# Moving the third sum of a Strassen group's tiles from VectorE to GpSimd, in a streaming-encoder block on one core

## The chip, the cores and the metric

The kernel runs on one core of one Trainium2 chip. The metric is device time in microseconds (us), the median of several runs. A core has five engines that run side by side and wait for each other through semaphores: TensorE (PE, with its weight loads PEld) multiplies matrices, VectorE (DVE) and ScalarE (ACT) work on tiles, GpSimd (POOL) does so too and issues some of the DMAs, SyncE (SP) issues the others. "128x1024" is a tile of 128 partitions by 1024 elements.

## The reference

One block of an encoder on 256 frames of width 2048, everything in float32: a half-step feed-forward layer, two token mixers beside each other (chunked attention and retention) merged by gates, a second half-step feed-forward layer, and a last norm.

```python
x = x + 0.5 * swiglu_ffn(rmsnorm(x, g1), ffn1_w_gate, ffn1_w_up, ffn1_w_down)   # 2048 -> 5632 -> 2048
h = rmsnorm(x, gm);  proj = h @ w_in                                             # 2048 -> 11264, nine parts
att = chunked_band_attention(q_a, k_a, v_a, rel_bias)
ret = silu(g_r) * chunkwise_retention(rotary(q_r), rotary(k_r), v_r)
merged = sigmoid(gate_a) * (att @ w_out_att) + sigmoid(gate_r) * (ret @ w_out_ret)
x = x + merged @ w_out
x = x + 0.5 * swiglu_ffn(rmsnorm(x, g2), ffn2_w_gate, ffn2_w_up, ffn2_w_down)
out = rmsnorm(x, gf)
```

## The kernel before

**Products in three parts.** Weights are streamed once, in chunks of 256 rows by 512 columns (`raw`, a 128x1024 tile). To keep float32 accuracy on TensorE, `split` makes two tiles of each chunk: `hi`, a rounded copy (ScalarE, line 126), and `lo`, the rest `raw - hi` (VectorE, line 127). `three` then multiplies hi by both parts of the activations (lines 137 and 138) and lo by the high part (line 140). So each chunk costs ScalarE one cast and VectorE one subtraction, and TensorE can't end the chunk's products before lo is there. At most four chunks (`SPLIT_BUFS`) are split ahead of TensorE.

**Strassen groups.** Two weight blocks of the same shape (the gate and up columns of a feed-forward block, or two gates of the mixer) are worked on together as 2 by 2 block matrices, in a form that spends 7 block products instead of 8 and pays for it with sums of weight chunks. There are 23 such groups: 9 in each feed-forward layer, 5 in the mixer. In a trace their tiles are named by a number: `z166k`, `z166x`, `loz16613s` belong to group 166. A group has four pairs of kept tiles, `k` and `x`, one pair for each of four slices `jc` of the inner dimension. Both are loaded by DMAs that GpSimd issues (line 539). The group goes through four phases. In phase 0 VectorE makes the first sum, x = x + k (line 528); in phase 1 the second, x = x + raw (line 583), where raw is a new chunk; then x is split (cast and subtraction, `hiz..1.s` and `loz..1.s`), and `third()` makes the third sum, k = x - k (line 570). After that GpSimd issues a DMA that loads one more chunk and adds it to x in memory (line 571), which becomes the x of phase 3. Phase 2 splits k, phase 3 splits x.

**Order.** The kernel writes its instructions in an order of its own (`weave`): steps of the groups alternate with chunks of ordinary products (`lo<-raw,hi` without a number), by shares written in a table. Each engine runs its instructions in that order and waits where a semaphore isn't there yet. Nothing reorders at run time. `third()` stands in `prep` of a phase 1 step, right behind the split of x.

Of the kernel before, what the change touches and what calls it, by code (L numbers as in the profile page):

```python
# [72 lines left out]
def block_kernel(ctx: ExitStack, tc: tile.TileContext, x, g1, w1g, w1u, w1d, gm, w_in, rel, woa, wor, wo,  # L73
                 g2, w2g, w2u, w2d, gf, cos, sin, decay, ident, out):
    nc = tc.nc
# [33 lines left out]
    def weights_tile(name):  # L109
        return wpool.tile([P, KC, NB], F32, tag="raw", bufs=RAW_BUFS, name=name)  # L110

    def chunk(w, r0, c0):
        return w[r0 : r0 + KC * P, c0 : c0 + NB].rearrange("(k p) n -> p k n", p=P)

    def fetch(t, w, r0, c0, parts=(slice(0, KC),)):
        for p in parts:
            nc.sync.dma_start(t[:, p, :], chunk(w, r0, c0)[:, p, :])
# [6 lines left out]
    def split(raw, name):  # L124
        hi, lo = split_tiles(name)
        nc.scalar.copy(hi, raw)  # L126
        nc.vector.tensor_sub(lo, raw, hi.bitcast(F32))  # L127
        return hi, lo
# [3 lines left out]
    def three(products, read_between=False):  # L132


        more = {"skip_group_check": True} if read_between else {}
        for acc, (ahi, alo), (whi, _), first, _ in products:
            nc.tensor.matmul(acc, ahi, whi, start=first, stop=False, **more)  # L137
            nc.tensor.matmul(acc, alo, whi, start=False, stop=False, **more)  # L138
        for acc, (ahi, _), (_, wlo), _, last in products:
            nc.tensor.matmul(acc, ahi, wlo, start=False, stop=last, **more)  # L140
# [372 lines left out]
    class Strassen:  # L513
# [43 lines left out]
        def step(self, phase, jc, of_sum):  # L557
            made = {}
            name = f"{self.name}{phase}{jc}{'rs'[of_sum]}"
            n = HALF_K // KC  # L560

            def load():
                made["raw"] = weights_tile(f"raw{name}")
                i = 2 - phase
                fetch(made["raw"], self.w[i], self.rows(1, jc), self.col[i])

            def third():

                x, k = self.x[jc], self.kept[jc]
                nc.vector.tensor_sub(k, x, k)  # L570
                nc.gpsimd.dma_start(x, chunk(self.w[0], self.rows(1, jc), self.col[0]), accum_op=ALU.add)

            def prep():
                x = self.x[jc]
                if not of_sum:
                    if phase == 0:
                        made["w"] = split(self.kept[jc], name)
                        self.first(jc)
                        return
                    raw = made.pop("raw")  # L580
                    made["w"] = split(raw, name)
                    if phase == 1:
                        nc.vector.tensor_add(x, x, raw)
                elif phase == 2:
                    made["w"] = split(self.kept.pop(jc), name)
                elif phase == 3:
                    made["w"] = split(self.x.pop(jc), name)
                else:
                    made["w"] = split(x, name)
                    if phase == 1:  # L590
                        third()

            bank, form, fresh, closing = {
# [4 lines left out]
            }[phase, of_sum]  # L598

            def products():  # L600
                hi, lo = made["w"]
                if fresh and jc == 0:
                    self.bank(bank)
                three([
                    (
                        self.acc[bank], self.norm.form(form, KC * jc + i), (hi[:, i, :], lo[:, i, :]),
                        fresh and jc == 0 and i == 0, closing and jc == n - 1 and i == KC - 1,
                    )
                    for i in range(KC)
                ], True)  # L610
                if jc == n - 1:
                    self.end(phase, of_sum)

            loaded = not of_sum and phase in (1, 2)
            frees = ["raw"] if loaded else ["kept"] if of_sum and phase > 1 else []
            return Step(self, 0, load if loaded else None, prep, frees, products)
# [641 lines left out]
```

## Time and profile before

| what | value |
|---|---|
| median of 3 runs | 2061.78 us (2060.89 to 2064.99) |
| the profiled execution | 2063.49 us, its span from first to last instruction 2061.4 us |
| TensorE clock granted | 0.999 of full speed |
| VectorE, ScalarE, GpSimd busy | 1754.4, 1402.9, 273.3 us |
| instructions of VectorE and GpSimd shown as busy | 1824 and 322 |
| the third sums, line 570 | 92 on VectorE, about 1.22 us each |

Times in a trace are counted from the first instruction. A row of the timeline gives the start, the duration, the engine, the line and the tiles as out<-in; "[4.44 <-DVE z166k L570]" says that the engine was idle for 4.44 us before it and that the instruction named ended that wait. Successive instructions of VectorE overlap a little: a 128x1024 sum is shown as 1.22 us, and the next one starts 1.13 to 1.14 us after it.

### The profile page before, as it was taken

What the parts mean: (1) busy time and instruction counts of PE and PEld (TensorE: products, weight loads), DVE (VectorE), ACT (ScalarE), POOL (GpSimd) and SP (SyncE); (2) the same over time, 40 slices, a digit from 0 to 9 for tenths busy, and PEclk for the clock granted to TensorE, in tenths of its full rate; (3) what the DMA queues carried; (4) which work ended last, traced back from release to release, by engine and by line L of the source; (5) the groups of instructions that cost most, each with busy time, mean ns of one, the idle gap of its engine ahead of it and who ended that gap; (6) DMA issues with size and microseconds to landing.
All of it is one profiled execution on the core that took longest, in us unless ns stands there. A gap on an engine that the chain in (4) does not pass through costs nothing.

```text
span 2061.4 us, 26148 instructions
## 1 busy us (share of the span) xinstructions
PE 2045.3 (99%) x9256; PEld 1691.9 (82%) x9256; DVE 1754.4 (85%) x1824; ACT 1402.9 (68%) x1732; POOL 273.3 (13%) x322
## 2 busy tenths in 40 slices
PE   9999999999999999999999999999999999999998
PEld 7788888888888888888888888888888878888886
DVE  7998899899997799899966667568989988998986
ACT  7677667777777767776665434556776677677785
POOL 1111211122111110122100000010122012110200
PEclk9999999999999999999999999999999999999999
DMA  8776876788678777788775645575787668876873
GB/s 308 207 225 230 269 227 207 239 264 258 191 231 258 240 205 251 258 284 260 227 267 175 223 143 187 187 245 170 235 273 234 200 224 273 240 206 233 281 215 133
DMA packets 219315, 473.28 MB, mean 230 GB/s; under 512 B 14816, under 2 KB 15568, under 8 KB 219184
## 3 DMA queue, kind: packets, MB, share of 16 engines
q1 hardware_dynamic: 161088, 309.89, 44.7%
q0 software_dynamic: 54752, 155.88, 27.9%
q10 hardware_dynamic: 3344, 5.84, 0.8%
q8 instruction: 72, 1.18, 0.2%
q14 instruction: 59, 0.48, 0.1%
HBM read 462.65 MB, written 8.91 MB: 229 GB/s over the span
## 4 chain that ended last, share of the span: by engine, by line
PE 93%; DVE 3%; DMA 2%; ACT 1%; issue 1%; SPq 0%; DVEq 0%; POOLq 0%; POOL 0%; ACTq 0%
PE acc L140 17%; PE acc L137 17%; PE acc L138 17%; DMA raw<-in_ffn_w_down_dram 2%; DVE lo L127 1%; ACT hi L126 0%; PE z684a L140 0%; PE z380a L137 0%; PE z953a L138 0%; PE z684a L138 0%; PE z418a L137 0%; PE z723a L138 0%; PE z380a L140 0%; PE z281a L138 0%; PE z723a L137 0%
## 5 line engine op out<-in xcount | busy, mean ns | idle before, releaser
L127 DVE TENSOR_TENSOR lo<-raw,hi 128x1024 fp32r<-128x1024 f32 x399 | 487.1, 1224 | 179.1 <-ACT hi L126 174.3
L126 ACT CAST hi<-raw 128x1024 fp32r<-128x1024 f32 x399 | 417.7, 1050 | 226.8 <-PE acc L138 143.7
L775 ACT ACTIVATE acc<-xall 128x512 f32<-128x512 f32 x96 | 57.5, 599 | 8.0 <-DVE f1g L742 3.6
L778 ACT ACTIVATE xall<-acc 128x512 f32<-128x512 f32 x96 | 56.6, 589 | 9.2 <-PE acc L140 7.4
L137 PE MATMUL acc<-hi,mgh 128*128 128x512 f32 x128 | 50.2, 392 | 0.0
L138 PE MATMUL acc<-hi,mgl 128*128 128x512 f32 x128 | 49.9, 390 | 0.0
L137 PE MATMUL acc<-hi,nma01h 128*128 128x512 f32 x96 | 38.7, 403 | 0.0
L137 PE MATMUL acc<-hi,nma00h 128*128 128x512 f32 x96 | 38.6, 402 | 0.0
L138 PE MATMUL acc<-hi,nma00l 128*128 128x512 f32 x96 | 37.5, 391 | 0.0
L137 PE MATMUL acc<-hi,nma10h 128*128 128x512 f32 x96 | 37.5, 391 | 0.0
L138 PE MATMUL acc<-hi,nma01l 128*128 128x512 f32 x96 | 37.5, 390 | 0.0
L138 PE MATMUL acc<-hi,nma11l 128*128 128x512 f32 x96 | 37.5, 390 | 0.0
L137 PE MATMUL acc<-hi,nma11h 128*128 128x512 f32 x96 | 37.4, 390 | 0.0
L138 PE MATMUL acc<-hi,nma10l 128*128 128x512 f32 x96 | 37.4, 390 | 0.0
L140 PE MATMUL acc<-lo,mgh 128*128 128x512 f32 x128 | 35.6, 390 | 0.0
L140 PE MATMUL acc<-lo,nma01h 128*128 128x512 f32 x96 | 29.6, 390 | 0.0
L140 PE MATMUL acc<-lo,nma00h 128*128 128x512 f32 x96 | 29.6, 390 | 0.0
L140 PE MATMUL acc<-lo,nma11h 128*128 128x512 f32 x96 | 29.6, 390 | 0.0
L140 PE MATMUL acc<-lo,nma10h 128*128 128x512 f32 x96 | 29.6, 390 | 0.0
L140 PEld LDWEIGHTS acc<-lo,mgh 128*128 128x128 f32 x128 | 24.0, 188 | 5.0
L137 PEld LDWEIGHTS acc<-hi,mgh 128*128 128x128 f32 x128 | 24.1, 188 | 4.9
L138 PEld LDWEIGHTS acc<-hi,mgl 128*128 128x128 f32 x128 | 24.1, 188 | 4.8
(6130 smaller groups left out, 6933.7 us busy)
## 6 DMA issues: line engine op xcount, KB each, us to landing
raw<-in_ffn_w_down_dram SPq DMA_DIRECT2D x176, 512.0 KB, 6.1
raw<-in_w_in_dram SPq DMA_DIRECT2D x96, 512.0 KB, 4.7
raw<-in_ffn_w_up_dram SPq DMA_DIRECT2D x32, 512.0 KB, 10.2
raw<-in_w_out_dram SPq DMA_DIRECT2D x32, 512.0 KB, 4.0
raw<-in_ffn_w_gate_dram SPq DMA_DIRECT2D x31, 512.0 KB, 5.9
raw<-in_w_out_att_dram SPq DMA_DIRECT2D x16, 512.0 KB, 4.3
raw<-in_w_out_ret_dram SPq DMA_DIRECT2D x16, 512.0 KB, 4.0
z380x<-in_w_in_dram POOLq DMA_DIRECT2D x8, 512.0 KB, 7.4
```

Source lines behind the costliest of these rows:

```text
L126: nc.scalar.copy(hi, raw)
L127: nc.vector.tensor_sub(lo, raw, hi.bitcast(F32))
L137: nc.tensor.matmul(acc, ahi, whi, start=first, stop=False, **more)
L138: nc.tensor.matmul(acc, alo, whi, start=False, stop=False, **more)
L140: nc.tensor.matmul(acc, ahi, wlo, start=False, stop=last, **more)
L775: nc.scalar.activation(acc, xs[t][:, cols], AF.Copy, scale=2.0)
L778: nc.scalar.activation(xs[t][:, cols], acc, AF.Copy, scale=0.5)
```

## The change

The third sum is given to GpSimd. It is the same subtraction on the same tiles, in the same place of the program.

```diff
             def third():

                 x, k = self.x[jc], self.kept[jc]
-                nc.vector.tensor_sub(k, x, k)
+                nc.gpsimd.tensor_sub(k, x, k)
                 nc.gpsimd.dma_start(x, chunk(self.w[0], self.rows(1, jc), self.col[0]), accum_op=ALU.add)
```

VectorE's order in phase 1 of group 166, its end (z166x and z166k are the group's kept tiles, the numbers behind them the buffers; loz1661.s the low parts of x, loz1661.r and rawz1661.r the new chunk; lo and raw a chunk of ordinary products):

```order
 L127 TENSOR_TENSOR loz16611s<-z166x_2702,hiz16611s 128x1024
-L570 TENSOR_TENSOR z166k_2690<-z166x_2702,z166k_2690 128x1024
 L127 TENSOR_TENSOR loz16613r<-rawz16613r,hiz16613r 128x1024
 L583 TENSOR_TENSOR z166x_2777<-z166x_2777,rawz16613r 128x1024
 L127 TENSOR_TENSOR lo_3061<-raw_2964,hi_3060 128x1024
 L127 TENSOR_TENSOR loz16612s<-z166x_2745,hiz16612s 128x1024
-L570 TENSOR_TENSOR z166k_2732<-z166x_2745,z166k_2732 128x1024
 L127 TENSOR_TENSOR loz16613s<-z166x_2777,hiz16613s 128x1024
-L570 TENSOR_TENSOR z166k_2759<-z166x_2777,z166k_2759 128x1024
 L127 TENSOR_TENSOR lo_3103<-raw_2978,hi_3102 128x1024
```

The sums are gone from VectorE's row and nothing takes their place; what stands behind each moves up.

GpSimd's order at the same place (L539 are loads of kept tiles, L571 the loads that add to x, z205k the next group's first kept tile):

```order
 L539 DMA z166x_2777<-in_ffn_w_gate_dram 128x2x512
+L570 TENSOR_TENSOR z166k_2616<-z166x_2642,z166k_2616 128x1024
 L571 DMA z166x_2642<-in_ffn_w_up_dram 128x2x512
+L570 TENSOR_TENSOR z166k_2690<-z166x_2702,z166k_2690 128x1024
 L571 DMA z166x_2702<-in_ffn_w_up_dram 128x2x512
+L570 TENSOR_TENSOR z166k_2732<-z166x_2745,z166k_2732 128x1024
 L571 DMA z166x_2745<-in_ffn_w_up_dram 128x2x512
+L570 TENSOR_TENSOR z166k_2759<-z166x_2777,z166k_2759 128x1024
 L571 DMA z166x_2777<-in_ffn_w_up_dram 128x2x512
 L539 DMA z205k_3174<-in_ffn_w_up_dram 128x2x512
```

Each sum now stands right ahead of the load that overwrites its x, and behind the load of the slice before. A sum on GpSimd needs x from line 583 only; the load behind it waits, as before, also for the cast and the subtraction that split x. The row of TensorE's instructions is the same in both kernels.

## The prediction

> **What bounds the kernel.** I read the page first (busy times, the chain that ended last), then the busy times by stage, then what TensorE waits for, then the timeline of VectorE around the sums. From the page:
>
> ```profile
> PE 2045.3 (99%) x9256; PEld 1691.9 (82%) x9256; DVE 1754.4 (85%) x1824; ACT 1402.9 (68%) x1732; POOL 273.3 (13%) x322
> ...
> PE 93%; DVE 3%; DMA 2%; ACT 1%; issue 1%; SPq 0%; DVEq 0%; POOLq 0%; POOL 0%; ACTq 0%
> ```
>
> TensorE is busy for 99% of the span and carries 93% of the chain. By stages, the Strassen groups lie in these (the first number behind the window is its length, then PE, PEld, DVE, ACT, POOL busy, the clock, the DMA share and GB/s); the last row is the 22 us around the sums of one group:
>
> ```profile
> 60.00:90.00 30.00, 28.39 (x125) 22.14 (x124) 30.00 (x29) 19.58 (x22) 6.30 (x7) 1.00 0.77 191
> 90.00:350.00 260.00, 259.94 (x1165) 214.86 (x1164) 239.05 (x222) 183.82 (x209) 39.21 (x46) 1.00 0.76 236
> 350.00:735.00 385.00, 384.25 (x1732) 317.63 (x1731) 337.83 (x337) 286.27 (x370) 59.28 (x69) 1.00 0.76 238
> 735.00:1035.00 300.00, 300.00 (x1337) 248.77 (x1336) 273.36 (x245) 210.85 (x226) 49.23 (x54) 1.00 0.83 254
> 1420.00:1990.00 570.00, 568.57 (x2543) 469.93 (x2542) 523.92 (x482) 408.98 (x472) 92.59 (x104) 1.00 0.78 237
> ...
> 337.00:359.00 22.00, 22.00 (x99) 18.22 (x98) 22.00 (x21) 15.41 (x18) 4.52 (x4) 1.00 0.87 235
> ```
>
> Two things are to be seen. TensorE is idle for only 1.61 + 0.06 + 0.75 + 0 + 1.43 = 3.85 us in all of these stages, so a lighter VectorE can give back about that. And around the sums VectorE is busy for 22.00 of 22.00 us: there it has no room at all. A busy TensorE may still be held up a little, since its ends are modelled; the waits of its weight loads show that better:
>
> ```profile
> PEld acc L140 <- DVE lo L127: 4.0, 8, 0.9
> PEld acc L137 <- ACT hi L126: 2.4, 3, 1.6
> ```
>
> These 6.4 us are the most that I allow as a gain. The timeline of VectorE in group 166, and the TensorE instruction that uses the last `lo` shown:
>
> ```profile
> 337.07 1.22 DVE L583 TENSOR_TENSOR z166x<-z166x,rawz16610r 128x1024 f32<-128x1024 f32 x1
> ...
> 341.61 1.22 DVE L127 TENSOR_TENSOR loz16610s<-z166x,hiz16610s 128x1024 fp32r<-128x1024 f32 x1
> 342.75 1.22 DVE L570 TENSOR_TENSOR z166k<-z166x,z166k 128x1024 f32<-128x1024 f32 x1
> 343.88 1.22 DVE L127 TENSOR_TENSOR loz16612r<-rawz16612r,hiz16612r 128x1024 fp32r<-128x1024 f32 x1
> ...
> 356.36 1.23 DVE L570 TENSOR_TENSOR z166k<-z166x,z166k 128x1024 f32<-128x1024 f32 x1
> 357.50 1.23 DVE L127 TENSOR_TENSOR lo<-raw,hi 128x1024 fp32r<-128x1024 f32 x1
> ...
> 359.16 0.62 PE L140 MATMUL acc<-lo,f1a1h 128*128 128x512 f32 x2
> ```
>
> From the first sum at 342.75 to the last at 356.36 every VectorE instruction is a subtraction or sum of two 128x1024 tiles in SBUF, one behind the other. The `lo` that starts at 357.50 ends at 358.73 and TensorE uses it at 359.16: VectorE is 0.43 us ahead. I call this distance the lead and looked for the shortest lead in and just behind the sums of each of the 23 groups. It is 1.99 us in the best (group 51), 0.05 in the worst, and 0.44 in the last; here the best, the first and the last:
>
> ```profile
> 147.54 1.23 DVE L127 TENSOR_TENSOR lo<-raw,hi 128x1024 fp32r<-128x1024 f32 x1
> 150.76 0.62 PE L140 MATMUL acc<-lo,f1a9h 128*128 128x512 f32 x2
> ...
> 74.21 1.22 DVE L127 TENSOR_TENSOR lo<-raw,hi 128x1024 fp32r<-128x1024 f32 x1
> 75.49 0.50 PE L140 MATMUL acc<-lo,n1a00h 128*128 128x512 f32 x1 [0.46 <-DVE lo L127]
> ...
> 1985.62 1.23 DVE L127 TENSOR_TENSOR lo<-raw,hi 128x1024 fp32r<-128x1024 f32 x1
> 1987.29 0.62 PE L140 MATMUL acc<-lo,f2a6h 128*128 128x512 f32 x2
> ```
>
> (147.54 + 1.23 = 148.77, used at 150.76: 1.99.) Over the 23 groups the shortest leads add up to 15.8 us, 0.69 on average. So whatever makes VectorE later by more than 0.69 us in a group's sums is paid by TensorE.
>
> **What the change removes.** 92 sums of VectorE. Each holds the next instruction back by 1.13 to 1.14 us (341.61, 342.75, 343.88 above); I take 1.135. That is 4.54 us in each group, 104 us in all. Taken alone it is worth little, because TensorE has only 3.85 to 6.4 us of waiting to give back. The largest piece lies in group 800, where the chain runs through a sum and a DMA that is issued late:
>
> ```profile
> 1647.39 1.09 DVE z800k L570
> ...
> 1650.82 11.20 DMA raw<-in_ffn_w_down_dram
> ```
>
> **What it adds on GpSimd.** The trace has no 128x1024 sum there. The nearest rows:
>
> ```profile
> L312 POOL MEMSET warm<- 128x512 f32 x1 | 0.5, 524 | 0.3 <-POOLq L1244 0.3
> ...
> L314 POOL MEMSET mhalf<- 128x4 f32 x1 | 0.1, 97 | 0.0
> ...
> L1115 POOL TENSOR_TENSOR frs<-v,mhalf 128x1 f32<-128x1 f32 x2 | 1.1, 559 | 66.2 <-DVE v L1113 66.2
> ...
> L373 POOL TENSOR_TENSOR rs<-v,mhalf 128x4 f32<-128x4 f32 x4 | 4.0, 1012 | 54.4 <-DVE v L372 54.4
> ```
>
> The fills give (524 - 97) / 508 = 0.84 ns for each element that passes. The powers of two inputs give (1012 - 559) / 3 = 151 ns for an element and 559 - 151 = 408 ns of start; the 151 belong to a power, I keep the start. Lower end: one element at a time at the speed of a fill, 0.86 + 0.10 = 0.96 us. Upper end: two reads and a write of each element one after the other, 2.58 + 0.41 = 2.99 us. I take two reads one after the other, 2 x 0.86 + 0.41 = 2.13 us, since the write can run beside the reads. [...]
>
> **GpSimd's queue.** The sums stand in front of the loads of line 571, and behind them the next group's loads:
>
> ```profile
> L571 POOL DMA_DIRECT2D z166x<-in_ffn_w_up_dram x4: 1194/1208/1240, 344.5 to 358.1; - x4
> ...
> z166x<-in_ffn_w_up_dram POOLq DMA_DIRECT2D x4, 512.0 KB, 6.4
> ...
> 360.72 1.06 ACT L126 CAST hiz16620s<-z166k 128x1024 fp32r<-128x1024 f32 x1 [0.58 <-PE acc L138]
> ...
> 372.99 1.04 ACT L126 CAST hiz16623s<-z166k 128x1024 fp32r<-128x1024 f32 x1
> ...
> 381.19 1.04 ACT L126 CAST hiz16633s<-z166x 128x1024 fp32r<-128x1024 f32 x1
> ```
>
> A slice costs GpSimd 2.13 + 1.21 = 3.34 us. The first sum may start at 338.3, when its x is done (337.07 + 1.22), and the last about where VectorE made it, near 356; its load is issued by about 359 and lands 6.4 us later, near 366. The last k is read at 372.99 and the last x at 381.19. So GpSimd may be some 15 us late before anyone waits. I cost its queue at nothing; without that cover each late us would go to ScalarE's cast and from there to TensorE.
>
> **Do the two engines hinder each other?** This decides the sign. Only one row has a GpSimd instruction of two inputs beside a VectorE one of two inputs:
>
> ```profile
> 19.38 1.23 DVE L127 TENSOR_TENSOR lo<-raw,hi 128x1024 fp32r<-128x1024 f32 x1
> 19.87 0.80 POOL L807 TENSOR_TENSOR there<-n1x,mhalf 128x4 f32<-128x4 f32 x1 [18.57 <-ACT n1x L462]
> ```
>
> A product of four elements takes 0.80 us and ends at 20.67, 0.06 us after the VectorE instruction (20.61). That is what a wait for VectorE's end would look like; it is one case, and start-up alone accounts for 0.41 us. Bounds of what a sum costs VectorE in waiting: 0 if they don't hinder each other, the whole sum if only one of them may read. I take the whole, 2.13 us, because this row is the only one of its kind. [...]
>
> **The sum.** A third sum then takes 1.135 us off VectorE and holds it up for 2.13: 0.995 later, 3.98 in a group. Less the shortest lead of each group that is 23 x 3.98 - 15.8 = 76 us. Four groups have a few VectorE instructions among the sums that read PSUM, or a pause of about 1 us; for a sum that falls there I take off 1 us each, 72 remain. The profiled execution (2063.5, that is 2.1 us around its span) is 1.7 above the median, 2061.8. So 2135.5 by its own time, 2134 beside the median. Ends of this case: with reads of 1.72 + 0.10 the group loses 2.74 and the sum is 47 us (2109); with 2.99 it is 155 (2217).
>
> **The rivals.**
> [...]
> - They don't hinder each other, and it gets faster. Speaking for it: the VectorE instruction at 19.38 kept its usual 1.23 us. TensorE then gets its 3.85 to 6.4 us back, group 800's late DMA first: 2055.4 to 2058. It decides at 1.135 us of waiting per sum: below that VectorE wins in every group, above it loses.
> - VectorE, which starts an instruction before the last one has ended, keeps GpSimd out until it pauses. The sums are pushed behind the cluster; the first k is due at 360.72, so ScalarE waits there for one sum, at most 2.13 us a group or 49 in all, less the lead that VectorE gained. 2060 to 2110.
>
> That the sums stay on VectorE is excluded by the order.
>
> **Chances.** Blocking 0.45 (2134, its own range 2100 to 2165), shared port 0.25 (2063 to 2099), no hindrance 0.18 (2055 to 2060), GpSimd kept out 0.12 (2060 to 2110). This kernel's runs can tell about 0.2%, 4 us, from no change. Faster by more: 0.14 of the third case and 0.01 of the last, 0.15. Within: 0.04, 0.05 of the shared port and 0.03 of the last, 0.12. Slower: 0.73. The range 2058 to 2165 leaves out most of the gain below and the long sums above, together about 0.2.
>
> **What would show it.** Line 570 has 92 rows on GpSimd of about 2.1 us, longer where they wait for VectorE. VectorE's lines 127 and 583 beside them are stretched to about 3.3 us or stand idle before; the lead is zero at the end of each group's sums, and TensorE waits for `lo` there, some 3 us a group, nothing elsewhere. [...] If line 570 takes over 3 us without waiting, only the size is wrong.

## The result, and the profile after

The changed kernel takes 2204.72 us (median of 4 runs, 2203.42 to 2206.36) against 2062.57 for the kernel before, a ratio of 1.0687 (95% interval 1.0672 to 1.0702). It is slower by 142 us. The sign was forecast; the time lies above the range of 2058 to 2165.

The page of the changed kernel, busy times, the chain that ended last, and the group of the ordinary chunks' `lo`; behind it the same group of the kernel before:

```profile
PE 2088.2 (95%) x9256; PEld 1704.7 (77%) x9256; DVE 1896.6 (86%) x1732; ACT 1400.8 (64%) x1732; POOL 590.1 (27%) x414
...
PE 81%; DVE 10%; issue 6%; DMA 1%; ACT 1%; DVEq 0%; ACTq 0%; POOLq 0%; POOL 0%
...
L127 DVE TENSOR_TENSOR lo<-raw,hi 128x1024 fp32r<-128x1024 f32 x399 | 562.6, 1413 | 174.4 <-ACT hi L126 168.3
```

```profile
L127 DVE TENSOR_TENSOR lo<-raw,hi 128x1024 fp32r<-128x1024 f32 x399 | 487.1, 1224 | 179.1 <-ACT hi L126 174.3 <-PE z684b L138 2.7 <-PE ro L981 1.0
```

VectorE has 92 instructions fewer (1824 to 1732) and is busy 142 us longer (1754.4 to 1896.6). TensorE falls to 95%, and VectorE's share of the chain grows from 3% to 10%. The same subtraction at line 127 takes 1413 ns on average instead of 1224. By stages:

```profile
90.00:350.00 260.00, 247.06 (x1076) 201.70 (x1075) 239.12 (x190) 169.00 (x191) 96.70 (x61) 0.98 0.75 226
350.00:735.00 385.00, 364.36 (x1577) 295.76 (x1576) 346.13 (x273) 261.73 (x312) 117.05 (x81) 0.98 0.72 215
735.00:1035.00 300.00, 283.85 (x1268) 231.12 (x1266) 276.89 (x234) 199.35 (x248) 99.48 (x65) 1.00 0.75 226
```

TensorE, which was idle for 0.06 us between 90 and 350, is now idle for 12.9 there, and the granted clock (the column behind POOL) is 0.98 in two of the stages. What it waits for:

```profile
PEld acc L140 <- DVE lo L127: 108.7, 60, 4.4
PE acc L140 <- DVE lo L127: 84.2, 50, 4.0
```

It waits for `lo`, as forecast: its weight loads do so 60 times instead of 8, for 108.7 us instead of 4.0. VectorE around the sums of group 166, and then GpSimd:

```profile
362.76 1.22 DVE L127 TENSOR_TENSOR loz16611r<-rawz16611r,hiz16611r 128x1024 fp32r<-128x1024 f32 x1
363.90 3.45 DVE L583 TENSOR_TENSOR z166x<-z166x,rawz16611r 128x1024 f32<-128x1024 f32 x1
367.27 1.21 DVE L127 TENSOR_TENSOR lo<-raw,hi 128x1024 fp32r<-128x1024 f32 x1
...
369.54 1.21 DVE L127 TENSOR_TENSOR loz16612r<-rawz16612r,hiz16612r 128x1024 fp32r<-128x1024 f32 x1
370.68 4.27 DVE L583 TENSOR_TENSOR z166x<-z166x,rawz16612r 128x1024 f32<-128x1024 f32 x1
374.87 1.21 DVE L127 TENSOR_TENSOR lo<-raw,hi 128x1024 fp32r<-128x1024 f32 x1
```

```profile
362.99 3.27 POOL L570 TENSOR_TENSOR z166k<-z166x,z166k 128x1024 f32<-128x1024 f32 x1 [25.16 <-ACT hi L126]
370.17 1.24 POOL L571 DMA_DIRECT2D z166x<-in_ffn_w_up_dram  x1 [3.91 <-DVE loz16610s L127]
370.95 2.90 POOL L570 TENSOR_TENSOR z166k<-z166x,z166k 128x1024 f32<-128x1024 f32 x1
```

The first sum waits for the VectorE instruction under way (it ends at 363.98) and runs to 366.26, 2.28 us. The next VectorE instruction shows 3.45 us instead of 1.22 and ends 1.09 us behind the sum (367.35). So it did nothing while the sum ran. At the second sum it is the same, with 4.27 us. Over the kernel 91 VectorE instructions of 128x1024 are stretched like this, by 246 us in all, 2.68 us for each of the 92 sums. That the sums saved 104 us and cost 246 is the 142 us by which VectorE is busier.

The stretches come in two sizes. The 23 sums that have no load of line 571 right in front of them stretch VectorE by 2.21 us (median), the 69 that stand right behind one by 2.99. In 64 of these 69 the stretched instruction had begun before the sum is recorded (0.27 us before, at 370.68). The loads by themselves stretch nothing: the kernel before issues the same 92, and none of its 128x1024 sums and subtractions takes more than 1.24 us.

### The profile page after: what moved, and what is told of

Read it like the earlier page. It is cut to its first block, busy times and chain, and to the rows that moved or that the text cites. A ratio compares the mean times of both kernels' runs of the same rounds, so it can differ in the third digit from the quotient of the medians.

```text
span 2201.8 us, 26159 instructions
## 1 busy us (share of the span) xinstructions
PE 2088.2 (95%) x9256; PEld 1704.7 (77%) x9256; DVE 1896.6 (86%) x1732; ACT 1400.8 (64%) x1732; POOL 590.1 (27%) x414
## 4 chain that ended last, share of the span: by engine, by line
PE 81%; DVE 10%; issue 6%; DMA 1%; ACT 1%; DVEq 0%; ACTq 0%; POOLq 0%; POOL 0%
PE acc L140 16%; PE acc L137 14%; PE acc L138 14%; DVE lo L127 5%; DMA raw<-in_ffn_w_down_dram 1%; DMA rawz53123r<-in_w_in_dram 1%; ACT hi L126 0%; PE z800a L140 0%; PE z281a L138 0%; PE z281a L137 0%; PE z128a L140 0%; PE z166a L137 0%; PE z166a L138 0%; PE z418a L138 0%; PE z418a L137 0%
## 5 line engine op out<-in xcount | busy, mean ns | idle before, releaser
L127 DVE TENSOR_TENSOR lo<-raw,hi 128x1024 fp32r<-128x1024 f32 x399 | 562.6, 1413 | 174.4 <-ACT hi L126 168.3
L570 POOL TENSOR_TENSOR z380k<-z380x,z380k 128x1024 f32<-128x1024 f32 x4 | 24.3, 6079 | 31.6 <-ACT hi L126 31.6
L570 POOL TENSOR_TENSOR z89k<-z89x,z89k 128x1024 f32<-128x1024 f32 x4 | 25.5, 6366 | 23.2 <-ACT acc L775 23.2
L140 PEld LDWEIGHTS acc<-lo,nma01h 128*128 128x128 f32 x96 | 17.5, 188 | 17.1 <-DVE lo L127 13.8
```

Source lines behind the costliest of these rows:

```text
L570: nc.gpsimd.tensor_sub(k, x, k)
```

## Experiments

SBUF holds the kernel's tiles; `acc` and the other sums that TensorE makes stand in PSUM. Theory A, on which the forecast rests: VectorE can't read two SBUF inputs while a GpSimd instruction reads SBUF. Theory B: the time goes because GpSimd itself is late with k and x. Theory C: any traffic of GpSimd to SBUF slows VectorE. Times of "before" are from the same chip and set of runs. Where an edit adds a line, the lines behind it are numbered one higher (584 for 583).

**The sum left out.**

```diff
-                nc.vector.tensor_sub(k, x, k)
```

> The third sum is left out (k keeps its old value, so phase 2 multiplies another chunk). The rest is as before. Every theory says the same: VectorE loses 92 times 1.135 us of work and GpSimd gets none, so only TensorE's 3.85 to 6.4 us of waiting come back: 2055 to 2059. This is the most that any place for the sum can win.

Measured: 2057.49 us against 2062.72, ratio 0.9977 (0.9968 to 0.9986). About 5 us is all that relieving VectorE of these sums can bring.

**A further sum on GpSimd, VectorE keeps its own.**

```diff
                 nc.vector.tensor_sub(k, x, k)
+                nc.gpsimd.tensor_sub(x, x, x)
```

> VectorE keeps its third sum, GpSimd makes a further 128x1024 subtraction of x from itself behind it, 92 in all (x becomes zero, so phase 3 multiplies only the chunk that the load adds). Theory A, VectorE can't read its two inputs while a GpSimd instruction reads SBUF: each costs VectorE about 2.9 us, 11.6 in a group, less the leads (15.8 in all): some 250 us, about 2310, somewhat less where the sum finds a pause. Theory B, the time went because GpSimd is slow and its results and loads come late: the load of x is some 3 us later with about 15 us to spare, so no change, 2062. Theory C, any GpSimd traffic to SBUF slows VectorE: as A.

Measured: 2183.65 us, ratio 1.0584 (1.0566 to 1.0601). Theory B is out as the main cause: k stays with VectorE, only some 10 us of TensorE's delay stand behind casts that wait for a late load, and 121 us came on top. The size was half of what theory A was given, since this sum, which reads one tile twice, holds VectorE less: the stretches add up to 164 us, 1.8 each. Where the sum meets VectorE instructions that take one input from PSUM, the trace shows which ones collide (VectorE, then GpSimd):

```profile
1499.12 1.40 DVE L743 SCALAR_TENSOR_TENSOR f2g<-acc,n2rstd,f2g 128x512 f32<-128x512 f32 x2
1500.44 1.89 DVE L127 TENSOR_TENSOR loz68412r<-rawz68412r,hiz68412r 128x1024 fp32r<-128x1024 f32 x1
1502.25 1.21 DVE L584 TENSOR_TENSOR z684x<-z684x,rawz68412r 128x1024 f32<-128x1024 f32 x1
```

```profile
1499.36 1.89 POOL L571 TENSOR_TENSOR z684x<-z684x 128x1024 f32<-128x1024 f32 x1 [48.70 <-DVE z684k L570]
```

The two instructions of line 743 read `acc` from PSUM; they keep their usual 0.7 us each while the sum runs beside them. Over this run 15 such instructions (lines 743 and 633) stand beside a sum at work, and none takes more than 0.75 us. Only the subtraction of two SBUF tiles behind them is stretched, by 0.67 us; it ends 1.08 us behind the sum (1502.33 and 1501.25).

**A fill on GpSimd.**

```diff
                 nc.vector.tensor_sub(k, x, k)
+                nc.gpsimd.memset(x, 0.0)
```

> VectorE keeps its third sum, GpSimd fills x with zeros behind it, 92 fills of 128x1024 (phase 3 multiplies only the chunk that the load adds). A fill writes and reads nothing. Theory A (reading is what collides): no VectorE row is stretched, 2062. Theory B: 2062. Theory C (any traffic): a fill takes about 0.95 us, 92 x 0.95 less the leads = 72 us, about 2134.

Measured: 2064.01 us, ratio 1.0004 (0.9995 to 1.0013). The fills of one group and the group of `lo`:

```profile
L571 POOL MEMSET z51x<- x4: 952/954/1151, 140.0 to 153.9; 128x1024 f32 x4
```

```profile
L127 DVE TENSOR_TENSOR lo<-raw,hi 128x1024 fp32r<-128x1024 f32 x399 | 486.1, 1221 | 178.9 <-ACT hi L126 176.9 <-PE ro L982 1.0
```

92 fills of 0.95 us, and line 127 keeps 1221 ns (1224 in the kernel before); not one VectorE row is stretched. These fills, which only write, do not collide, so theory C is out.

**A copy on GpSimd, one input.**

```diff
                 nc.vector.tensor_sub(k, x, k)
+                nc.gpsimd.tensor_copy(x, x)
```

> VectorE keeps its third sum, GpSimd copies x onto itself behind it, 92 copies of 128x1024, one input each; nothing else changes. Theory A: VectorE waits for the length of the copy, which I put at 1.0 to 1.5 us: 92 x 1.0 to 1.5 less the leads = 76 to 122 us, 2138 to 2184. Theory B: 2062. Theory C: as A.

Measured: 2144.33 us, ratio 1.0397 (1.0382 to 1.0413), inside theory A's range, but partly by luck. One input is enough to collide: the stretches add up to 78 us. Less the leads that is 62 us, or 2125, below the range. The rest has another cause: of the 79.5 us by which the span grew, about 30 stand before products of the split of x in phase 3 and of the next group's first tiles, which wait for GpSimd's loads. The copies were kept out for up to 20 us by an unbroken row of VectorE instructions, and the loads behind them came late.

**Half of the sum on GpSimd.**

```diff
-                nc.vector.tensor_sub(k, x, k)
+                nc.vector.tensor_sub(k[:, 0, :], x[:, 0, :], k[:, 0, :])
+                nc.gpsimd.tensor_sub(k[:, 1, :], x[:, 1, :], k[:, 1, :])
```

> Each third sum is cut in two: VectorE makes the first 512 columns, GpSimd the other 512, 92 of each. Theory A with a hold in proportion to the size: VectorE loses 2.7 / 2 = 1.35 us and saves 0.57, 0.78 per sum, less the leads 56 us, about 2119. Theory A with a fixed part of about 1.1 us in each collision: it loses 0.8 + 1.1 = 1.9, saves 0.57, 1.33 per sum, less the leads 107 us, about 2170. If only GpSimd's lateness counted, half of it would be hidden: 2062.

Measured: 2143.25 us, ratio 1.0388 (1.0374 to 1.0402), between the two. The stretches tell why: a half sum that stands free costs VectorE 1.10 us, half of 2.21, so the sum's own hold goes with its size (16 of the 23; the other 7 were kept out for up to 21.6 us and stretch nothing). One right behind a load costs 1.93 (median of 69), most often 1.9 to 2.0. The fixed part, about 0.8 us in both sizes, comes only with the load.

**Only the last of the four sums on GpSimd.**

```diff
-                nc.vector.tensor_sub(k, x, k)
+                (nc.gpsimd if jc == 3 else nc.vector).tensor_sub(k, x, k)
```

> Only the last of a group's four third sums is made by GpSimd, 23 in all, the other three by VectorE. Theory A: each costs VectorE 2.7 to 3.05 us and saves 1.135, so 1.6 to 1.9 in a group against a shortest lead of 0.69 on average: 21 to 28 us, 2083 to 2091. If the cost came from four sums and four loads queueing behind each other on GpSimd, a single one would cost nothing: 2061 or less.

Measured: 2068.22 us against 2063.20, ratio 1.0025 (1.0016 to 1.0035). Both expectations missed. VectorE and GpSimd at the end of group 166's sums:

```profile
361.82 1.22 DVE L127 TENSOR_TENSOR loz16621r<-rawz16621r,hiz16621r 128x1024 fp32r<-128x1024 f32 x1
363.29 3.10 DVE L127 TENSOR_TENSOR lo<-raw,hi 128x1024 fp32r<-128x1024 f32 x1 [0.25 <-ACT hi L126]
```

```profile
360.47 4.83 POOL L570 TENSOR_TENSOR z166k<-z166x,z166k 128x1024 f32<-128x1024 f32 x1
```

The sum stands ready at 360.47, is kept out by two VectorE instructions, gets in where VectorE pauses for 0.25 us (363.04), and ends at 365.30. By then VectorE is about 3.4 us ahead of TensorE, and the stretch of 1.88 us is nearly covered. The 23 stretches add up to 44 us; only some 5 reach the end. All 23 of these sums stand right behind a load, but only 5 got in at once, and those stretch VectorE by 2.4 to 3.0 us. 17 were kept out, as the one shown, and hold it less.

**The sums ahead of all four loads.** (In the changed kernel.)

```diff
                 nc.gpsimd.tensor_sub(k, x, k)
-                nc.gpsimd.dma_start(x, chunk(self.w[0], self.rows(1, jc), self.col[0]), accum_op=ALU.add)
+                for j in range(n) if jc == n - 1 else ():
+                    nc.gpsimd.dma_start(self.x[j], chunk(self.w[0], self.rows(1, j), self.col[0]), accum_op=ALU.add)
```

> The four sums of a group on GpSimd as in the changed kernel, but its four loads that add to x are issued behind the last of them, so that no sum stands right behind a load. [...] Then every sum costs 2.2: 92 x 2.21 = 203, less 104 saved, less the leads 16 = 83 us, about 2146. Theory E: 3.0 us is the sum's own hold once VectorE is always busy, wherever the loads stand: unchanged, about 2205.

Measured: 2187.14 us, ratio 1.0604 (1.0588 to 1.0620). VectorE in group 166 (rows of 1.2 us left out), and GpSimd:

```profile
357.94 3.44 DVE L584 TENSOR_TENSOR z166x<-z166x,rawz16611r 128x1024 f32<-128x1024 f32 x1
...
362.44 3.42 DVE L127 TENSOR_TENSOR loz16610s<-z166x,hiz16610s 128x1024 fp32r<-128x1024 f32 x1
...
369.19 3.42 DVE L127 TENSOR_TENSOR loz16611s<-z166x,hiz16611s 128x1024 fp32r<-128x1024 f32 x1
```

```profile
361.52 3.26 POOL L570 TENSOR_TENSOR z166k<-z166x,z166k 128x1024 f32<-128x1024 f32 x1 [1.22 <-DVE z166x L584]
368.27 3.27 POOL L570 TENSOR_TENSOR z166k<-z166x,z166k 128x1024 f32<-128x1024 f32 x1 [3.49 <-DVE z166x L584]
...
378.22 4.95 POOL L572 DMA_DIRECT2D z166x<-in_ffn_w_up_dram  x4
```

Theory D, that the sum's own hold is 2.2 us and the rest of the 3.0 comes with the load in front, holds for the hold: 80 of the 92 sums now stretch VectorE by about 2.2 us, the others by less, none by 3.0, and the total falls from 246 to 191 us. The time fell by only 18 of the 59 us expected. TensorE's waits by what they stand in front of: some 77 us for `lo` (191 - 104 - 16 = 71 by the formula of the expectation), 15 for first tiles and casts that wait for loads, which are now bunched, and 28 more than before in slow starts, of which the next section speaks. Only about 9 of these 28 lie where the clock is low; most of the others are starts 0.33 to 0.36 us apart (131 instead of 17), the greater part at line 140.

**The sums three steps later, with their loads.**

```diff
                     if phase == 1:
-                        third()
+                        later(3, third)
```

> As the changed kernel, but each sum with its load stands three steps later in the program. The hold is the same (theory A, 2.2 to 3.0 us per sum), but it falls partly where VectorE's lead is 2 to 4 us or where it pauses: less than 2205 by up to 2.5 us a group, 2150 to 2190. If the place doesn't matter: 2205.

(The sum is on GpSimd here.) Measured: 2205.11 us against 2061.94, ratio 1.0688 (1.0671 to 1.0706). My expectation missed: the stretches add up to 248 us, as without the delay, and no more of them was hidden. Why the lead that a single sum could use does not help four was not tried apart.

**VectorE's own sums, put later.** Two kernels, without sums on GpSimd: the third and fourth sum, with their loads, three steps later, and the last three sums, with theirs, five steps later.

```diff
-                        third()
+                        later(3, third) if jc > 1 else third()
```

> No sum on GpSimd. The third and fourth third sums of a group stay on VectorE but are put three steps later, behind the stretch where its lead is shortest. If the lead there is what binds, it grows by up to 2.27 us and most of the 3.85 to 6.4 us of waiting go: 2057 to 2060. If the waits only move to the later place: 2062.

```diff
-                        third()
+                        later(5, third) if jc else third()
```

> As the kernel with two deferred sums, but three of the four third sums are put five steps later. If the lead binds: 2056 to 2059, as with the sums left out; if five steps later VectorE is as short of time: 2062 or more.

Measured: 2060.01 us against 2063.20, ratio 0.9984 (0.9975 to 0.9993), and 2061.68, ratio 0.9991 (0.9983 to 1.0000). The first is the one version here that computes everything and is clearly faster than the kernel before, by 3 of the 5 us that there are; the second can't be told from no change. What remains in the first of the weight loads' wait for `lo`, 4.0 us before:

```profile
PEld acc L140 <- DVE lo L127: 2.5, 5, 0.9
```

## Why the forecast failed, step by step

The mechanism and the sign were right; the size of the hold was not, and with it the time fell out of the range.

**What bounds the kernel: right.** TensorE had 3.85 to 6.4 us to give back; with the sums left out 5 came.

**What the change removes: right.** 92 sums, 104 us of VectorE.

**The two engines hinder each other: right, on thin evidence.** I took the whole sum as the price because of one row of four elements; beyond that row, the 0.45 that I gave it was my estimate. The extra sum and the copy (stretches of 164 and 78 us), the fill (none) and the PSUM rows (at most 0.75 us each) show that what collided here was GpSimd reading SBUF with VectorE reading two SBUF inputs. VectorE waited until the whole GpSimd instruction had ended: the stretched row ends 1.09 us behind the sum (367.35 and 366.26), about the 1.135 us that a whole one takes. The signs that I named came, only larger: VectorE's rows are stretched to 3.4 and 4.2 us instead of about 3.3, and TensorE waits some 4.7 us in a group for `lo` instead of 3.

**The hold of 2.13 us: the term that was mis-sized.** For a free sum it was good: 2.21 us. The extra copy at 1477.89, beside VectorE instructions that read PSUM, took 1.04 us with its read and its write, a fill, which only writes, 0.95: the write ran beside the read. No run shows the two reads and the start of 0.41 us apart. But only 23 of the 92 sums are free. The other 69 stand right behind a load that GpSimd is still issuing, and hold VectorE 2.99 us. The mean is 2.68, and by my own formula 23 x 4 x (2.68 - 1.135) - 15.8 gives 126 us instead of 76, which would have been 2188, still above the range. (The upper end of my bounds, 2217, has the measured time below it, but the range left it out. It also used 2.99 us, for three passes over each element; that the sums behind a load show the same figure is chance.)

**"I cost its queue at nothing": the step that failed.** I asked whether the sums would make the loads late and found 15 us of cover; that held, since in the changed kernel no cast of ScalarE shows a wait for one of these loads. I did not ask what a load in front does to a sum: it adds about 0.8 us of hold to 69 of them, and with the loads moved away none holds VectorE for more than 2.3.

**The leads of 15.8 us: too simple.** VectorE became 142 us longer, and TensorE's waits for `lo` grew by some 108. More was absorbed than the shortest leads allow, perhaps in part because a kept-out sum falls on a pause, as with the single sum; that was not shown for four sums.

**A cost that was not in the sum.** Successive products start 0.227 us apart here (five of them from 155.62 to 156.53 in the changed kernel). After a long pause they often didn't at once. TensorE by stages around one long wait, in the changed kernel (length, PE busy, clock, DMA share, GB/s), and the row where it ends:

```profile
150.00:155.00 5.00, 5.00 (x24) 1.00 0.60 150
155.00:160.00 5.00, 1.92 (x9) 1.00 0.75 140
160.00:165.00 5.00, 4.29 (x12) 0.66 1.12 267
```

```profile
160.71 1.11 PE L140 MATMUL acc<-lo,f1a9h 128*128 128x512 f32 x2 [3.79 <-DVE lo L127]
```

It waits 3.79 us for `lo`; in the 5 us from 160 on the granted clock is 0.66 on average and it starts 12 products instead of 24. The half clock lasts 3.4 us (from 160.86), and there are 12 such stretches of 3.4 or 6.8 us before the last instructions, none in the kernel before. In the 3.4 us ahead of each of the 12, TensorE had been idle for at least 1.85. Starts 0.43 us apart number 101 (4 before), 90 of them in these stretches. Slow starts of all kinds cost 29 us more than before, about 19 of it in the stretches of half clock; the others are mostly starts 0.33 to 0.36 us apart (73 instead of 17), the greater part at line 140. So the 140 us by which the span grew are about 108 of waiting for `lo` and 29 of slow starts. Part of the slow starts may have been idle time in any case, so the 19 are an upper bound of what the clock alone cost.

Put together, beside the 76 us of the forecast: 50 more for the longer holds, 18 less because more was absorbed than the leads said, and 29 more for the slow starts make 137 of the 140.

**The rivals.** No hindrance, the rival on the other side, is excluded by the stretched rows. That VectorE loses only a part of the sum's time, the 2063 to 2099 of the chances, is excluded by them too, since they end 1.09 us behind the sum, about what a whole row takes. GpSimd kept out until VectorE pauses occurred in part: 11 of the 92 sums show 5.5 to 16.9 us.

```profile
L570 POOL TENSOR_TENSOR z89k<-z89x,z89k x4: 2830/2882/16872, 214.6 to 240.5; 128x1024 f32<-128x1024 f32 x4
L570 POOL TENSOR_TENSOR z166k<-z166x,z166k x4: 2850/2876/3270, 363.0 to 386.8; 128x1024 f32<-128x1024 f32 x4
```

The columns are shortest, median and longest of four. All 11 are the first sum of their group, with no load in front. The moment does not decide it: the other 12 first sums, which got in behind the VectorE instruction under way, start at the same place beside it, 0.90 to 0.92 us before the next one. Nor does a load in front, since with the last sum alone on GpSimd 17 of 23 sums behind a load were kept out too. What decides whether a sum gets in between two VectorE instructions or waits through ten of them stays open.

## What to carry to other kernels

Where VectorE works through instructions of two SBUF inputs without a pause, and the instruction moved to GpSimd reads SBUF, count the GpSimd instruction's whole duration as VectorE time, and compare it with what is saved: here 2.2 to 3.0 us against 1.1. Beside the VectorE instructions here that take an input from PSUM, and for a fill, nothing was lost; other kinds were not tried. Look at what stands in front of the moved instruction on its new engine, not only at what stands behind it. And before moving work off an engine, ask how much the bound engine waits for it: here 5 us in 2062, most of which a shift of two sums by three steps gave back.

## What the runs showed of the hardware that I had not expected

- A sum on GpSimd that stands right behind a DMA issue on GpSimd's own queue and gets in at once held VectorE longer than the same sum alone: 2.99 us against 2.21 for the sum of 1024 elements, 1.93 against 1.10 for 512 (medians). With the loads moved away the extra is gone (at most 2.3 us). The trace fits a hold that begins while the load's issue is still going on (370.17 to 371.41 in group 166, with the sum recorded from 370.95), but that was not measured by itself.
- VectorE instructions of two SBUF inputs that follow each other without a pause kept GpSimd out for 10 us and more: the longest records are 16.9 us (sums of two tiles), 20 us (copies) and 21.6 us (half sums), the work itself included.
- A fill of 128x1024 on GpSimd, 0.95 us, cost VectorE nothing: line 127 kept 1221 ns, against 1224 before.
- TensorE's granted clock fell to one half for 3.4 or 6.8 us at 12 places beside its waits (one of 3.79 us is shown; the least idle time in the 3.4 us ahead of one was 1.85 us), in a kernel whose mean clock had been 0.999. Not every long wait did it: one of 2.91 us, which ended at 950.89, was not followed by such a stretch.
